# A hybrid decoder block on one core: recurrence gates as 64-row products, pooling by a scan, the mixer's scale on ScalarE

## The chip, the core and the metric

The kernel runs on one NeuronCore of a Trainium2 chip. A core has a matmul engine (TensorE, PE in the profile, with PEld for its weight loads), VectorE (DVE), ScalarE (ACT), GpSimd (POOL) and SyncE (SP), which here issues DMAs. Matmuls write to PSUM, from which VectorE and ScalarE read; everything else lies in SBUF, 128 partitions wide. The metric is the time of one launch in microseconds (us) on the device.

## The reference

One layer on x of 1024 tokens by 1024 channels, in float32. The projection `proj` (1536 columns) is cut into a pooling part (512), a recurrent part (512) and a gate branch (512):

```python
z = rms_norm(h, norm_mix_g[l]); proj = z @ w_in[l]
# pooling: four groups of 128 channels, trailing means over w = 2, 4, 8, 16 tokens
outs.append((c - c_lag) / count[None, :, None] - ug[:, :, g])      # c: running sum, c_lag: the same w tokens ago
y = jnp.einsum('bsgc,gcd->bsgd', d, pool_w) + pool_b
return y.reshape(B, S, D_POOL) * pool_scale
# recurrence: 8 heads of 64 channels, after a causal convolution of 4 taps
r = sigmoid(einsum('bshi,hij->bshj', uh, gate_a_w) + gate_a_b)
i = sigmoid(einsum('bshi,hij->bshj', uh, gate_x_w) + gate_x_b)
a = exp(LRU_C * r * log_sigmoid(lru_L)); b = sqrt(1 - a*a) * (i * u)   # h[t] = a[t] h[t-1] + b[t]
```

Then come `w_out` on both parts, an MLP of 4096 with squared ReLU, a gated embedding (`w_ple_gate`, `w_ple_proj`) and a final norm.

## The kernel before, in words

Channels lie on partitions and tokens along the free axis, so a tile is 128 channels by 1024 tokens. Every product is made of three matmuls per 128x128 block and 512 tokens: each operand is split into a high and a low part (`split`: ScalarE writes the high part, VectorE the low one), and `mm` runs high x high, high x low, low x high.

The stages in order of time: the norm and the first three projections (`ps_l`), nine more projections of eight blocks each (`ps_i`, by `project`, 48 matmuls each), with the gates (`ps_g`, `lru_gates`) and the mixer (`ps_p`, `pool_mix`) between them, the output projection (`ps_o`), the MLP (`ps_P`, by a Strassen-like scheme), and the gated embedding (`ps_e`, `ps_j`).

The recurrence works on four tiles `o` of 128 channels, two heads each, in two pairs. `conv` makes the tile `H[o]` and its split `B[4 + o]`. `lru_gates(pair)` multiplies it by the gate weights, which lie block-diagonally in 128x128 blocks (the two heads' 64x64 blocks, zeros elsewhere), once for gate a and once for gate x, and ScalarE takes the sigmoid of each from PSUM. `lru_scan` makes a and b of them (Exp, Tanh, Square, Sqrt on ScalarE) and runs the recurrence as one scan on VectorE. `pool_windows(g)` adds a tile to itself shifted by 1, 2, 4, 8 until the window is full.

PSUM has eight banks of 512 columns. `psum()` hands them out in turn: odd calls take a tile of 1024 columns from a pool of two (`pp`), even calls two banks of a pool of four (`pd`). A tile is reused once all of its readers are done, so a product waits for the readers of the one two of its kind before. The order on each engine is that of a scheduler which places the instructions of the program text; each engine then runs its own list strictly in order, held by semaphores. `LSETS` are the scratch tiles for the gates: first a's place (`ct`, gate x before that), then r (`rt`, gate a).

Weights come by DMA into `raw` tiles and are split ahead of use (`weights`, one block ahead); the small gate and mixer weights go through the two tiles `hl`.

Of the kernel before, what the change touches and what calls it, by code (L numbers as in the profile page):

```python
# [7 lines left out]
F32 = mybir.dt.float32  # L8
F32R = mybir.dt.float32r
AF = mybir.ActivationFunctionType  # L10
ALU = mybir.AluOpType

P = 128
S = 1024
D = 1024
DFF = 4096
HALF = 512
# [11 lines left out]
NLRU = 4  # L29
NPOOL = 4  # L30
# [7 lines left out]
COLS = {}  # L38
# [11 lines left out]
def block_kernel(  # L50
# [16 lines left out]
    nc = tc.nc  # L67
    pool = ctx.enter_context(tc.tile_pool(name="pool", bufs=1))
# [10 lines left out]
    T = [t_all[:, i] for i in range(6)]  # L79
# [10 lines left out]
    def space(name, n, dt, side="left"):  # L90

        spaces[name] = ExitStack()
        sb = spaces[name].enter_context(tc.tile_pool(name=name, bufs=1, side=side))
        return [sb.tile([P, S], dt, name=f"{name}{i}") for i in range(n)]
# [4 lines left out]
    def pairs(tiles):  # L99
        return list(zip(tiles[::2], tiles[1::2]))  # L100
# [13 lines left out]
    B = pairs(space("y", 12, F32R)) + pairs(space("y2", 4, F32R, "right"))  # L114

    def bank(name):
        return pd.tile([P, HALF], F32, tag="pd", name=name)

    def banks(name):
        return pp.tile([P, S], F32, tag="pp", name=name)  # L120
# [4 lines left out]
    def hl(i):  # L125
        return small[i // 2][:, HALVES[i % 2]]
# [3 lines left out]
    def psum(name, one=False):  # L130

        turn.append(name)
        if one or len(turn) % 2 == 1:
            return [(slice(0, S), banks(name))]
        return [(hs, bank(f"{name}_{hs.start}")) for hs in HALVES]

    def f32(ap):
        return ap.bitcast(F32)

    def col(name, i):  # L140
        c = COLS[name] + i
        return vecs[:, c : c + 1]
# [6 lines left out]
    def split(src, hi, lo, g=None, eng=None):  # L149

        if g is None:
            pin(nc.scalar.activation(hi, src, AF.Copy))  # L152
            pin((eng or nc.vector).tensor_tensor(lo, src, f32(hi), ALU.subtract))  # L153
        else:
            pin(nc.scalar.activation(hi, src, AF.Identity, scale=g))
            pin(nc.vector.scalar_tensor_tensor(lo, src, g, f32(hi), ALU.mult, ALU.subtract))  # L156
# [148 lines left out]
    def small_weights(name, raw):  # L305
        hi, lo = hl(2), hl(3)
        split(raw, hi, lo)
        return hi, lo

    def mm(parts, whi, wlo, zhi, zlo, first, last, only=None, more=False, held=False):  # L310
        outs = [
            (slice(hs.start + n, hs.start + min(n + HALF, w)), ps[:, n : min(n + HALF, w)])
            for hs, ps in parts
            for w in (hs.stop - hs.start,)
            for n in range(0, w, HALF)
            if only is None or hs.start + n == only.start
        ]
        for w, z in ((whi, zhi), (whi, zlo), (wlo, zhi)):
            for hs, ps in outs:
                ins = nc.tensor.matmul(  # L320
                    ps, w, z[:, hs],
                    start=first and z is zhi and w is whi,
                    stop=last and w is wlo,
                    skip_group_check=more,
                )
                if held:
                    tc.keep_in_program_order(ins)
                    held = False

    def kblk(t, k):  # L330
        return t[:, k * P : (k + 1) * P]


    vecs = pool.tile([P, NVEC], F32, name="vecs")
# [4 lines left out]
    ones_f = f32(ones)  # L339
# [3 lines left out]
    class Norm:  # L343
# [53 lines left out]
        def rstd(self, out, parts=None):  # L397


            for hs, o in parts or self.sums():  # L400
# [6 lines left out]
                nc.vector.reciprocal(few, few)  # L407
                nc.vector.transpose(r, few.unsqueeze(2).broadcast_to([P, n, 32]))

    def tables():  # L410

        one = ones_f[:, :16]
        tc.keep_in_program_order(
            nc.vector.tensor_tensor_scan(recip_t, one, one, 0.0, ALU.mult, ALU.add)
        )
        nc.vector.reciprocal(recip_t, recip_t)


        tc.keep_in_program_order(nc.vector.memset(T[5], 0.0))
        rv = T[5].rearrange("p (n a t c) -> p n a t c", n=2, a=2, t=2)  # L420
        for pair in range(2):
            for a in range(2):
                for par in range(2):
                    r = slice(64 * par, 64 * par + 64)
                    nc.sync.dma_start(rv[r, pair, a, :, r], gates[pair, a, par])


    norm = Norm("n0", T[0], T[1:3])
# [50 lines left out]
    def project(i):  # L479

        whi, wlo = weights()
        ps = psum(f"ps_i{i}")
        for k in range(NT):
            mm(ps, kblk(whi, k), kblk(wlo, k), *A[k], k == 0, k == NT - 1)
        return ps

    def normed(dst, parts):
        for hs, ps in parts:
            nc.vector.tensor_tensor(dst[:, hs], ps, R[:, hs], ALU.mult)

    def conv(o, ps):
        u, xb = (H[6], T[4])[o % 2], H[o]
        normed(u, ps)
        nc.scalar.activation(
            xb, u, AF.Identity, bias=col("conv_b", o), scale=col("conv_w", 4 * o + TAPS - 1)
        )
        for j in range(1, TAPS):
            nc.vector.scalar_tensor_tensor(
                xb[:, j:], u[:, : S - j], col("conv_w", 4 * o + TAPS - 1 - j), xb[:, j:],
                ALU.mult, ALU.add,  # L500
            )
        split(xb, *B[4 + o])

    LSETS = ((H[4], H[5], H[6]), (H[7], T[3], T[4]))

    gate_w, mix_w = {}, {}

    def ask_gates(pair):
        gate_w[pair] = small_weights(f"gw{pair}", T[5][:, pair * HALF : (pair + 1) * HALF])

    def ask_mix():
        raw = wp.tile([P, S], F32, tag="raw", name="pw_raw")[:, :HALF]
# [2 lines left out]

    def lru_gates(pair):

        hi, lo = gate_w[pair]
        for t in range(2):
            o = 2 * pair + t  # L520
            ct, rt, _ = LSETS[t]
            for a, (dst, b) in enumerate(((rt, "ga_b"), (ct, "gx_b"))):
                ps = psum(f"ps_g{a}{o}")
                mm(ps, kblk(hi, 2 * a + t), kblk(lo, 2 * a + t), *B[4 + o], True, True)
                for hs, part in ps:
                    nc.scalar.activation(dst[:, hs], part, AF.Sigmoid, bias=col(b, o))
            nc.vector.tensor_tensor(H[o], H[o], ct, ALU.mult)

    def lru_scan(pair):
# [23 lines left out]
    def pool_windows(g, ps):  # L553
        w = WINDOWS[g]
        u, *st = T[:3]
        if ps:
            normed(u, ps)
        cur, step, n = u, 1, 0
        while step < w:
            nxt = st[n % 2]  # L560
            nc.vector.tensor_tensor(nxt[:, step:], cur[:, step:], cur[:, : S - step], ALU.add)
            nc.vector.tensor_copy(nxt[:, :step], cur[:, :step])
            cur, step, n = nxt, 2 * step, n + 1
        nc.vector.tensor_tensor(cur[:, : w - 1], cur[:, : w - 1], recip_t[:, : w - 1], ALU.mult)
        nc.vector.tensor_tensor(cur[:, : w - 1], cur[:, : w - 1], u[:, : w - 1], ALU.subtract)
        nc.vector.scalar_tensor_tensor(
            cur[:, w - 1 :], cur[:, w - 1 :], 1.0 / w, u[:, w - 1 :], ALU.mult, ALU.subtract
        )
        split(cur, *B[g])

    def pool_mix(pair):
        whi, wlo = mix_w[0]
        for t in range(2):
            g = 2 * pair + t
            ps = psum(f"ps_p{g}")
            mm(ps, kblk(whi, g), kblk(wlo, g), *B[g], True, True)
            for hs, part in ps:
                nc.vector.tensor_scalar(
                    T[5][:, hs], part, col("pool_b", g), col("pool_s", g), ALU.add, ALU.mult
                )  # L580
            split(T[5], *B[g])

    conv(0, ps_l[0])
    conv(1, ps_l[1])
    ask_gates(0)
    conv(2, ps_l[2])
    conv(3, project(0))
    pool_windows(0, project(1))
    lru_gates(0)
    ask_gates(1)  # L590
    pool_windows(1, project(2))
    ps = project(3)
    normed(T[0], ps)
    lru_scan(0)
    lru_gates(1)
    ask_mix()
    pool_windows(2, None)
    ps = project(4)
    pool_mix(0)
    pool_windows(3, ps)  # L600
    gate_out(0, project(5))
    lru_scan(1)
    gate_out(1, project(6))
    pool_mix(1)
    gate_out(2, project(7))
    gate_out(3, project(8))
# [3 lines left out]
    for o in range(NT):  # L610
        whi, wlo = weights()
        nc.sync.dma_start(H[o], xT[o * P : (o + 1) * P, :])
        ps = psum(f"ps_o{o}")
        for k in range(NT):
            mm(ps, kblk(whi, k), kblk(wlo, k), *B[k], k == 0, k == NT - 1)
        z = T[o % 2]
# [79 lines left out]
    for o in range(0, NT, 2):  # L696
        t = o // 2
        for i in range(2):
            split(H[o + i][:, FIRST], *half(B[t], i), col("g_mlp", o + i))
    for o in range(1, NT, 2):  # L700
        t = o // 2
# [412 lines left out]
```

## Time and profile before

| what | value |
|---|---|
| time, median of 3 runs | 976.52 us (976.5 to 977.01) |
| profiled execution, its own time | 977.54 us |
| its span, first to last instruction | 975.5 us |
| TensorE busy | 964.8 us (99%), 4472 matmuls |
| VectorE busy | 757.0 us (78%), 885 instructions |
| ScalarE busy | 442.7 us (45%), 528 instructions |
| GpSimd busy | 99.1 us (10%) |
| mean granted TensorE clock | 0.998 |

A row of the timeline gives the start in us from the span's start, the duration, the engine, the line of the kernel, the operation, output and input tiles, shape, and how many instructions were merged; in brackets stands the idle time before it and what ended that. A row of the chain gives start, duration, engine, tile and line. A row of the windows gives from:to, length, and for PE, PEld, DVE, ACT and POOL busy time and count, then granted clock, DMA share and GB/s.

### The profile page before, as it was taken

How to read it: one execution, taken by the hardware profiler on the slowest of the kernel's cores; microseconds unless marked ns; L12 is line 12 of the kernel's file. 1: busy time of each engine (PE TensorE's matmuls, PEld its weight loads, DVE VectorE, ACT ScalarE, POOL GpSimd, SP SyncE). 2: the span in 40 equal slices, each digit the busy share in tenths (PEclk: the TensorE clock that was granted, in tenths of full speed). 3: DMA queues.
4: the chain of work that ended last, by engine and by line, in shares of the span. 5: the costliest groups of instructions: out<-in, count | busy, mean ns of one | idle time of the engine just before them, and what ended most of it. 6: DMA issues, size and time to landing. Idle time of an engine off the chain costs nothing.

```text
span 975.5 us, 11507 instructions
## 1 busy us (share of the span) xinstructions
PE 964.8 (99%) x4472; PEld 805.2 (83%) x4472; DVE 757.0 (78%) x885; ACT 442.7 (45%) x528; POOL 99.1 (10%) x72
## 2 busy tenths in 40 slices
PE   9999999999999999999999999999999999999996
PEld 7888888888788888888888888888888888888996
DVE  7999995449887777677777899879775669784976
ACT  7377643336543343334333544444343337552534
POOL 0000000002523322332331000000000000000210
PEclk9999999999999999999999999999999999999999
DMA  6301243110245345434533897356532341031122
GB/s 231 105 23 33 87 151 107 45 43 30 82 152 201 119 140 177 159 119 160 196 119 137 307 368 254 110 194 202 174 118 90 108 151 44 3 127 44 44 87 87
DMA packets 46198, 125.04 MB, mean 128 GB/s; under 512 B 5312, under 2 KB 7360, under 8 KB 46144
## 3 DMA queue, kind: packets, MB, share of 16 engines
q1 hardware_dynamic: 46000, 124.27, 36.9%
q8 instruction: 35, 0.57, 0.2%
q14 instruction: 19, 0.16, 0.1%
q10 hardware_dynamic: 144, 0.04, 0.0%
HBM read 90.74 MB, written 33.55 MB: 127 GB/s over the span
## 4 chain that ended last, share of the span: by engine, by line
PE 95%; DVE 3%; ACT 1%; DMA 1%; issue 0%; SPq 0%; DVEq 0%
PE ps_P_u L320 31%; PE ps_P_d L320 31%; PE ps_i L320 10%; PE ps_o L320 9%; PE ps_e L320 8%; PE ps_l L320 3%; PE ps_g L320 1%; PE ps_j L320 1%; PE ps_p L320 1%; DVE h L968 1%; DMA h<-in_xT 1%; DVE a L153 1%; DVE a L156 0%; DVE t L984 0%; DVE wu_lo L153 0%
## 5 line engine op out<-in xcount | busy, mean ns | idle before, releaser
L320 PE MATMUL ps_P_d<-a,wd_P_hi 128*128 128x512 f32 x880 | 271.1, 389 | 0.0
L320 PEld LDWEIGHTS ps_P_d<-a,wd_P_hi 128*128 128x128 f32 x880 | 165.2, 188 | 34.4
L320 PE MATMUL ps_P_d<-a,wd_P_lo 128*128 128x512 f32 x440 | 171.3, 389 | 0.0
L320 PE MATMUL ps_P_u<-a,wu_hi 128*128 128x512 f32 x512 | 157.7, 389 | 0.0
L320 PE MATMUL ps_P_u<-y,wu_hi 128*128 128x512 f32 x384 | 118.1, 389 | 0.0
L320 PEld LDWEIGHTS ps_P_u<-a,wu_hi 128*128 128x128 f32 x512 | 96.1, 188 | 19.9
L659 DVE TENSOR_TENSOR t<-t,ps_P_u 128x512 f32<-128x512 f32 (+1 forms) x80 | 62.6, 784 | 47.9 <-PE ps_P_u L320 47.7
L320 PE MATMUL ps_P_u<-a,wu_lo 128*128 128x512 f32 x256 | 99.6, 389 | 0.0
L320 PEld LDWEIGHTS ps_P_d<-a,wd_P_lo 128*128 128x128 f32 x440 | 82.6, 188 | 17.4 <-DVE wd_P_lo L153 0.3
L320 PEld LDWEIGHTS ps_P_u<-y,wu_hi 128*128 128x128 f32 x384 | 72.1, 188 | 14.9
L320 PE MATMUL ps_i<-a,wi_hi 128*128 128x512 f32 x288 | 77.1, 389 | 0.0
L320 PE MATMUL ps_P_u<-y,wu_lo 128*128 128x512 f32 x192 | 74.8, 390 | 0.4 <-DVE wu_lo L153 0.4
L153 DVE TENSOR_TENSOR a<-wd,a 128x1024 fp32r<-128x1024 f32 x56 | 67.1, 1219 | 5.2 <-ACT a L152 4.1
L152 ACT ACTIVATE a<-wd 128x1024 fp32r<-128x1024 f32 x56 | 58.8, 1057 | 21.2 <-PE ps_P_d L320 10.2
L320 PE MATMUL ps_o<-y,wo_hi 128*128 128x512 f32 x256 | 68.4, 389 | 0.0
L320 PEld LDWEIGHTS ps_i<-a,wi_hi 128*128 128x128 f32 x288 | 54.1, 188 | 11.2
L152 ACT ACTIVATE wu_hi<-wu 128x1024 fp32r<-128x1024 f32 x24 | 25.5, 1062 | 78.3 <-PE ps_P_u L320 43.9
L152 ACT ACTIVATE wu_hi<-wu_raw 128x1024 fp32r<-128x1024 f32 (+1 forms) x25 | 25.3, 1011 | 78.2 <-PE ps_P_u L320 44.8
L320 PEld LDWEIGHTS ps_P_u<-a,wu_lo 128*128 128x128 f32 x256 | 48.0, 188 | 10.0
L320 PEld LDWEIGHTS ps_o<-y,wo_hi 128*128 128x128 f32 x256 | 48.0, 188 | 10.0
L152 ACT ACTIVATE wd_P_hi<-wd 128x1024 fp32r<-128x1024 f32 x24 | 25.4, 1060 | 58.2 <-PE ps_P_d L320 58.0
L153 POOL TENSOR_TENSOR wg_lo<-wg_raw,wg_hi 128x1024 fp32r<-128x1024 f32 x4 | 9.9, 2478 | 408.7 <-DVE h L953 382.1
(224 smaller groups left out, 1634.2 us busy)
## 6 DMA issues: line engine op xcount, KB each, us to landing
wd<-act SPq DMA_DIRECT2D x56, 512.0 KB, 5.6
act<-t SPq DMA_DIRECT2D x32, 512.0 KB, 4.3
wu_raw<-in_w_up SPq DMA_DIRECT2D x16, 512.0 KB, 3.7
wu<-in_w_up SPq DMA_DIRECT2D x16, 512.0 KB, 4.6
act<-wu SPq DMA_DIRECT2D x16, 512.0 KB, 4.5
wd<-in_w_down SPq DMA_DIRECT2D x16, 512.0 KB, 6.2
h<-in_xT SPq DMA_DIRECT2D x15, 512.0 KB, 4.3
wg_raw<-in_w_gate SPq DMA_DIRECT2D x12, 512.0 KB, 3.3
```

The lines of the kernel that those rows point to most:

```text
L152: pin(nc.scalar.activation(hi, src, AF.Copy))
L153: pin((eng or nc.vector).tensor_tensor(lo, src, f32(hi), ALU.subtract))
L320: ins = nc.tensor.matmul(ps, w, z[:, hs], start=first and z is zhi and w is whi, stop=last and w is wlo, skip_group_check=more,)
L659: (eng or nc.vector).tensor_tensor(to, to if y is None else y, x, ALU.add)
L968: nc.vector.scalar_tensor_tensor(hv, hv, col("g_fin", o), rfin[:, hs], ALU.mult, ALU.mult)
```

## The change

Three things. The gate weights are packed so that one 64-row product per head gives both gates: weights `[64 rows, 128 columns]` with gate a in one half of the columns and gate x in the other (swapped for the second head), so that the two heads of a tile use rows 0-63 and 64-127 of the array and write to two PSUM tiles. Each PSUM tile then holds gate a in 64 of its partitions and gate x in the others, so the sigmoids go by halves of 64 partitions. The weights need half the columns (512 for all eight heads), one DMA, no zeroing and one split. Pooling over 4, 8 and 16 tokens becomes a running sum by a scan: state + u[t] - u[t - w], after a short scan for the first w tokens. The mixer's `(x + b) * s` becomes `x * s + b * s` in one ScalarE instruction, with `b * s` made once.

```diff
+    pool_bs = pool.tile([P, NPOOL], F32, name="pool_bs")
...
-        tc.keep_in_program_order(nc.vector.memset(T[5], 0.0))
-        rv = T[5].rearrange("p (n a t c) -> p n a t c", n=2, a=2, t=2)
...
-                    nc.sync.dma_start(rv[r, pair, a, :, r], gates[pair, a, par])
+        nc.sync.dma_start(T[5][:, FIRST], gates)
+        nc.vector.tensor_tensor(pool_bs, vecs[:, c_b : c_b + NPOOL], vecs[:, c_s : c_s + NPOOL], ALU.mult)
...
+    HEADS = slice(0, 64), slice(64, P)
-    def ask_gates(pair):
-        gate_w[pair] = small_weights(f"gw{pair}", T[5][:, pair * HALF : (pair + 1) * HALF])
+    def ask_gates():
+        gate_w[0] = small_weights("gw", T[5][:, FIRST])
...
     def lru_gates(pair):
-        hi, lo = gate_w[pair]
+        hi, lo = gate_w[0]
         for t in range(2):
             o = 2 * pair + t
             ct, rt, _ = LSETS[t]
-            for a, (dst, b) in enumerate(((rt, "ga_b"), (ct, "gx_b"))):
-                ps = psum(f"ps_g{a}{o}")
-                mm(ps, kblk(hi, 2 * a + t), kblk(lo, 2 * a + t), *B[4 + o], True, True)
-                for hs, part in ps:
-                    nc.scalar.activation(dst[:, hs], part, AF.Sigmoid, bias=col(b, o))
+            zhi, zlo = B[4 + o]
+            ps = [psum(f"ps_g{h}{o}") for h in range(2)]
+            halves = [
+                [(hs.start + n, x[:, n : n + HALF]) for hs, x in parts for n in range(0, hs.stop - hs.start, HALF)]
+                for parts in ps
+            ]
+            for n, (w, z) in enumerate(((hi, zhi), (hi, zlo), (lo, zhi))):
+                for (at, x0), (_, x1) in zip(*halves):
+                    for r, x in zip(HEADS, (x0, x1)):
+                        nc.tensor.matmul(
+                            x, w[r, o * P : (o + 1) * P], z[r, at : at + HALF], start=n == 0, stop=n == 2
+                        )
+            for dst, b, rows in ((rt, "ga_b", HEADS), (ct, "gx_b", HEADS[::-1])):
+                for h, r in enumerate(rows):
+                    for hs, part in ps[h]:
+                        nc.scalar.activation(
+                            dst[HEADS[h], hs], part[r], AF.Sigmoid, bias=col(b, o)[r]
+                        )
...
-        cur, step, n = u, 1, 0
-        while step < w:
-            nxt = st[n % 2]
-            nc.vector.tensor_tensor(nxt[:, step:], cur[:, step:], cur[:, : S - step], ALU.add)
-            nc.vector.tensor_copy(nxt[:, :step], cur[:, :step])
-            cur, step, n = nxt, 2 * step, n + 1
+        cur = st[g % 2]
+        if w == 2:
...
+        else:
+            nc.vector.tensor_tensor_scan(cur[:, :w], ones_f[:, :w], u[:, :w], 0.0, ALU.mult, ALU.add)
+            nc.vector.tensor_tensor_scan(
+                cur[:, w:], u[:, w:], u[:, : S - w], cur[:, w - 1 : w], ALU.add, ALU.subtract
+            )
...
-                nc.vector.tensor_scalar(
-                    T[5][:, hs], part, col("pool_b", g), col("pool_s", g), ALU.add, ALU.mult
-                )
+                nc.scalar.activation(
+                    T[5][:, hs], part, AF.Identity, bias=pool_bs[:, g : g + 1], scale=col("pool_s", g)
+                )
...
     conv(1, ps_l[1])
-    ask_gates(0)
+    ask_gates()
...
     lru_gates(0)
-    ask_gates(1)
     pool_windows(1, project(2))
```

How instructions move, at the two places of the first gate pair. The first is ScalarE's list from the sigmoids of the first gate tile on. `ps_g_0`, `ps_g_512` are the two banks of a `pd` product, `ps_g` without such a number is a 1024-column product, `y_130` is the high part of the fourth convolved tile. Before:

```order
L526 ACTIVATE h<-ps_g_0_609,vecs 128x512 [waits PE_49]
L526 ACTIVATE h<-ps_g_512_610,vecs 128x512 [waits PE_49]
L526 ACTIVATE h<-ps_g_619,vecs 128x1024 [waits PE_49]
L526 ACTIVATE t<-ps_g_0_628,vecs 128x512 [waits PE_49]
L526 ACTIVATE t<-ps_g_512_629,vecs 128x512 [waits PE_49]
L152 ACTIVATE y_130<-h 128x1024 [waits DVE_49,Activation_49]
L526 ACTIVATE h<-ps_g_638,vecs 128x1024 [waits PE_49]
```

and in the changed kernel, the same place:

```order
L539 ACTIVATE h<-ps_g_0_603,vecs 64x512 [waits PE_49]
L539 ACTIVATE h<-ps_g_512_604,vecs 64x512 [waits PE_49]
L539 ACTIVATE h<-ps_g_605,vecs 64x1024 [waits PE_49]
L152 ACTIVATE y_130<-h 128x1024 [waits DVE_49,Activation_49]
L539 ACTIVATE h<-ps_g_0_603,vecs 64x512
L539 ACTIVATE h<-ps_g_512_604,vecs 64x512
L539 ACTIVATE h<-ps_g_605,vecs 64x1024
```

Each gate product is now read twice, and the second reading of the first one (`ps_g_0_603`, `ps_g_512_604`) stands behind the split into `y_130`. The second place is TensorE's list for the second gate tile of the pair and the start of the next projection. Before:

```order
L320 MATMUL ps_g_0_628<-y_123,hl_136 128x512
L320 MATMUL ps_g_512_629<-y_123,hl_136 128x512
L320 MATMUL ps_i_0_655<-a,wi_hi 128x512 [waits Activation_49]
L320 MATMUL ps_g_638<-y_123,hl_136 128x512 [waits DVE_49]
L320 MATMUL ps_g_638<-y_123,hl_136 128x512
L320 MATMUL ps_g_638<-y_124,hl_136 128x512 x2
L320 MATMUL ps_g_638<-y_123,hl_136 128x512 x2
L320 MATMUL ps_i_512_656<-a,wi_hi 128x512 [waits Activation_49]
```

and in the changed kernel:

```order
L533 MATMUL ps_g_0_625<-y_123,hl_136 128x512
L533 MATMUL ps_g_512_626<-y_123,hl_136 128x512
L533 MATMUL ps_g_627<-y_123,hl_136 128x512 [waits DVE_49]
L533 MATMUL ps_g_627<-y_123,hl_136 128x512
L533 MATMUL ps_g_627<-y_124,hl_136 128x512 x2
L533 MATMUL ps_g_627<-y_123,hl_136 128x512 x2
L320 MATMUL ps_i_0_653<-a,wi_hi 128x512 [waits PE_49,Activation_49]
```

In this tile the six matmuls of rows 0-63 (`ps_g_0_625`, `ps_g_512_626`) stand ahead of the six of rows 64-127 (`ps_g_627`); in the other three tiles the two halves alternate. The projection's first matmul no longer stands inside the gates.

More of the change, by code (lines that the diff above doesn't have):

```diff
@@ L408, in rstd @@
                 nc.vector.transpose(r, few.unsqueeze(2).broadcast_to([P, n, 32]))
+    pool_bs = pool.tile([P, NPOOL], F32, name="pool_bs")
+    c_b, c_s = COLS["pool_b"], COLS["pool_s"]
     def tables():
@@ L416, in tables @@
         nc.vector.reciprocal(recip_t, recip_t)
-        tc.keep_in_program_order(nc.vector.memset(T[5], 0.0))
-        rv = T[5].rearrange("p (n a t c) -> p n a t c", n=2, a=2, t=2)
[L421 to L424, printed above, removed]
-                    nc.sync.dma_start(rv[r, pair, a, :, r], gates[pair, a, par])
+        nc.sync.dma_start(T[5][:, FIRST], gates)
+        nc.vector.tensor_tensor(pool_bs, vecs[:, c_b : c_b + NPOOL], vecs[:, c_s : c_s + NPOOL], ALU.mult)
     norm = Norm("n0", T[0], T[1:3])
@@ L557, in pool_windows @@
             normed(u, ps)
-        cur, step, n = u, 1, 0
-        while step < w:
-            nxt = st[n % 2]
-            nc.vector.tensor_tensor(nxt[:, step:], cur[:, step:], cur[:, : S - step], ALU.add)
-            nc.vector.tensor_copy(nxt[:, :step], cur[:, :step])
-            cur, step, n = nxt, 2 * step, n + 1
+        cur = st[g % 2]
+        if w == 2:
+            nc.vector.tensor_tensor(cur[:, 1:], u[:, 1:], u[:, : S - 1], ALU.add)
+            nc.vector.tensor_copy(cur[:, :1], u[:, :1])
+        else:
[3 more added lines that the diff above has]
+            )
         nc.vector.tensor_tensor(cur[:, : w - 1], cur[:, : w - 1], recip_t[:, : w - 1], ALU.mult)
@@ L1071 @@
     conv = np.asarray(conv_w)[0].reshape(TAPS, NLRU, P).transpose(2, 1, 0).reshape(P, NLRU * TAPS)
+    gx_b = np.roll(cols(gate_x_b), 64, axis=0)
     vec = np.concatenate(
@@ L1074 @@
             cols(norm_mix_g), cols(norm_mlp_g), cols(norm_ple_g), cols(norm_final_g), cols(pool_b),
-            cols(pool_scale), conv, cols(conv_b), cols(gate_a_b), cols(gate_x_b), cols(lru_L),
+            cols(pool_scale), conv, cols(conv_b), cols(gate_a_b), gx_b, cols(lru_L),
             cols(b_ple_gate),
@@ L1079 @@
     )
-    gates = np.stack([np.asarray(g)[0].reshape(2, 2, 2, 64, 64) for g in (gate_a_w, gate_x_w)])
-    gates = gates.transpose(1, 0, 3, 4, 2, 5)
+    ga, gx = (np.asarray(g)[0].reshape(NLRU, 2, 64, 64) for g in (gate_a_w, gate_x_w))
+    gates = np.stack([np.stack([ga[:, 0], gx[:, 0]], 2), np.stack([gx[:, 1], ga[:, 1]], 2)])
+    gates = gates.transpose(0, 2, 1, 3, 4)
     wu = np.asarray(w_up)[0].reshape(NT // 2, 2, P, NPAIR, 2, P).transpose(3, 2, 4, 1, 0, 5)
@@ L1093 @@
         "pool_w": c(np.asarray(pool_w)[0].transpose(1, 0, 2)).reshape(P, NPOOL * P),
-        "gates": c(gates),
+        "gates": c(gates).reshape(P, NLRU * P),
         "w_out": tiles(np.asarray(w_out)[0]),
```

## Prediction

> **What bounds the kernel now.** I read the page first, then the waits of TensorE alone up to 250 us, then the chain that ended last, and last the timeline of the two places where the recurrence's gates are computed.
>
> ```profile
> PE 964.8 (99%) x4472; PEld 805.2 (83%) x4472; DVE 757.0 (78%) x885; ACT 442.7 (45%) x528; POOL 99.1 (10%) x72
> PE ps_l L320 <- DVE a L156: 0.3, 1, 0.3
> 62.53 4.08 PE ps_g L320 x18
> 66.83 1.36 PE ps_g L320 x6
> 68.19 21.53 PE ps_i L320 x95
> 89.73 5.44 PE ps_g L320 x24
> 95.17 10.88 PE ps_i L320 x48
> ```
>
> TensorE works 99% of the span, and up to 250 us its matmuls wait once for input data, 0.3 us at the start. The chain shows what it does in the region of the change: 24 gate matmuls for heads' pair 0 (62.5 to 68.2), two projections, 24 gate matmuls for pair 1, the next projection, with nothing between them. One 128x512 matmul takes 5.44/24 = 0.2267 us. So a microsecond less of TensorE there is worth one at the end, but only if TensorE doesn't begin to wait; and a wait that appears there is lost in full, since nothing later in the chain makes it up. The other engines in that stretch:
>
> ```profile
> 50.00:75.00 25.00, 25.00 (x112) 20.71 (x111) 25.00 (x27) 19.24 (x21) 0.00 (x0) 1.00 0.06 22
> 75.00:100.00 25.00, 25.00 (x112) 20.67 (x112) 23.81 (x28) 19.32 (x20) 0.00 (x0) 1.00 0.16 53
> ```
>
> VectorE (fourth column: 25.00, then 23.81 of 25 us) and ScalarE (19.2 of 25) are nearly full too. They run just ahead of TensorE, so the reader should expect that a faster gate product runs into one of them.
>
> **What leaves VectorE, and why it is worth nothing.**
>
> ```profile
> 112.00 1.22 DVE L561 TENSOR_TENSOR t<-t 128x1023 f32<-128x1023 f32 x1
> 113.14 1.22 DVE L153 TENSOR_TENSOR y<-t,y 128x1024 fp32r<-128x1024 f32 x1
> 87.04 2.29 DVE L544 TENSOR_TENSOR_SCAN h<-h 128x1024 f32<-128x1024 f32 x1
> 115.41 1.52 DVE L578 TENSOR_SCALAR t<-ps_p,vecs 128x512 f32<-128x512 f32 x2
> ```
>
> An add of 1023 columns occupies VectorE 1.14 us (112.00 to 113.14), a scan of 1024 2.29 us. Windows 4, 8 and 16 had 2, 3 and 4 adds (2.3, 3.4, 4.6 us, plus small copies) and now have one scan each, about 2.4 us with its short head: 0, 1.0 and 2.2 us less. The mixer's shift and scale, four tiles of about 1.4 us, go to ScalarE. That is some 9 us off VectorE, nearly all behind 96 us where TensorE waited for nothing: worth 0. So is the zeroing of the gate weights' tile and the eight small DMAs. The one gates DMA now stands on SP's queue ahead of the fourth x tile, but the wait it could cause has cover:
>
> ```profile
> 22.49 1.15 ACT L155 ACTIVATE a<-h,vecs 128x1024 fp32r<-128x1024 f32 x1 [1.21 <-DMA h<-in_xT]
> 31.44 1.28 DVE L383 TENSOR_TENSOR hl<-t,hl 128x512 fp32r<-128x512 f32 x2
> 35.56 0.40 PE L384 MATMUL n_ps<-hl,ones 128*128 128x512 f32 x1
> ```
>
> The last x tile lands at 22.5, its sums are split by 32.7 and TensorE takes them up at 35.6: 2.8 us of slack. I take 0, with 0.3 either way.
>
> **The gate products.** There are still 48 matmuls of 512 columns (12 for each of four tiles o), now with 64 rows each. Where they alternate between rows 0-63 and 64-127, two can run at once: 6 x 0.2267 = 1.36 us for a tile instead of 2.72. By the order of the built program this holds for three of the four: for the second tile of pair 0 all six of one half come first, then the six of the other. TensorE's own gain would be 3 x 1.36 = 4.1 us. The trace of before has no 64-row matmul. Its bounds are 0.2267 us for two (both run together) and 0.4534 (one after the other). Weight loads don't stand against the lower one:
>
> ```profile
> 916.83 2.90 PE L320 MATMUL ps_e<-a 128*128 128x256 f32 x24
> 919.57 0.39 PE L384 MATMUL n_ps<-ple,ones 128*128 128x512 f32 x1
> ```
>
> 24 matmuls of 256 columns, each with its own load, take 2.74 us, 0.114 each, so two loads fit in one 0.2267. I take the lower bound.
>
> **What gives it back.** A gate tile's bank is now read twice, because each bank holds 64 rows of both gates: eight 1024-column tiles become sixteen of 64 rows (24 ScalarE instructions for 12), and rows don't shorten an instruction that goes by columns. The projection that follows pair 0 (ps_i in two banks) takes over the first gate tile's banks. Before, their two readers were the first two of the sigmoids; now the last readers stand behind the split of y_130. ScalarE and VectorE there:
>
> ```profile
> 63.19 1.28 ACT L526 ACT_TABLE_LOAD   x1
> 64.49 2.27 ACT L526 ACTIVATE h<-ps_g,vecs 128x512 f32<-128x512 f32 x3
> 65.17 1.22 DVE L489 TENSOR_TENSOR t<-ps_i,rstd 128x1024 f32<-128x1024 f32 x1
> 66.31 1.27 DVE L498 SCALAR_TENSOR_TENSOR h<-t,vecs,h 128x1021 f32<-128x1021 f32 x1
> 66.64 1.27 ACT L526 ACTIVATE t<-ps_g,vecs 128x512 f32<-128x512 f32 x2
> 67.78 1.08 ACT L152 ACTIVATE y<-h 128x1024 fp32r<-128x1024 f32 x1
> 68.73 1.14 ACT L526 ACTIVATE h<-ps_g,vecs 128x1024 f32<-128x1024 f32 x1
> 254.28 0.50 PE L320 MATMUL ps_P_u<-y,wu_lo 128*128 128x512 f32 x1 [0.45 <-DVE wu_lo L153]
> 254.62 0.63 PE L320 MATMUL ps_P_u<-y,wu_hi 128*128 128x512 f32 x2
> ```
>
> Pair 0, step by step. The split of y_130 needs the last tap of the convolution, which VectorE ends at 66.31 + 1.27 = 67.58 in both kernels (its order up to there is the same). So the split starts at 67.60, the next sigmoid 0.95 later (67.78 to 68.73) at 68.55. A 512-column sigmoid lasts 0.70 (two starts 0.57 apart end after 1.27), so the first bank is free at 69.25. A matmul released by a wait starts 0.04 later and loses 0.11 (254.28 to 254.62 is 0.34 for one of 0.2267): as if it had started at 69.40. Before, the 96 matmuls up to 89.73 began in effect at 89.73 - 96 x 0.2267 = 67.97. **+1.43 us**, and not a function of how fast the gates are: done by 67.8 (the second half waits for a bank until VectorE has read ps_i at 66.39, then six matmuls), they wait 1.5 us.
>
> Pair 1 starts at T = 91.2. ScalarE before:
>
> ```profile
> 89.31 1.06 ACT L152 ACTIVATE wi_hi<-wi_raw 128x1024 fp32r<-128x1024 f32 x1 [1.14 <-PE ps_i L320]
> 90.39 1.28 ACT L526 ACT_TABLE_LOAD   x1
> 91.69 2.27 ACT L526 ACTIVATE h<-ps_g,vecs 128x512 f32<-128x512 f32 x3
> 93.84 1.28 ACT L526 ACTIVATE t<-ps_g,vecs 128x512 f32<-128x512 f32 x2
> 89.56 5.60 PE L320 MATMUL ps_g<-y,hl 128*128 128x512 f32 x24
> 91.50 1.22 DVE L489 TENSOR_TENSOR t<-ps_i,rstd 128x1024 f32<-128x1024 f32 x1
> ```
>
> The next projection again takes the first gate tile's banks, read first and fourth among the sigmoids. In the built program the table load itself now waits for the first bank's ninth matmul, which starts 4 x 0.2267 after T and ends 0.39 later: T + 1.30. Then 0.04, the load 1.28, three sigmoids 2.15 (91.69 to 93.84), the fourth 0.70, 0.04 and 0.11: T + 5.62, against 5.44 before. **+0.18 us.** The second tile needs another bank, which VectorE's read of the last projection (ps_i) frees: 91.50 + 1.22 = 92.7 before. It stands behind the scan that ScalarE feeds, and ScalarE now has 4.3 us of sigmoids more in pair 0, of which its gaps (it was 77% busy there) hide most; I expect it 1 to 2 us later. It takes over only from T + 4.2 = 95.4 on (six more matmul pairs of 1.36 us end at T + 5.6), and then a us costs a us.
>
> Changing between full and half height may add a gap in which the array runs empty. The nearest row is the tail of one matmul, 0.39 - 0.23 = 0.16 us; it counts only on entering pair 1 (elsewhere TensorE waits anyway). Bounds 0 and 0.16, I take 0.1. The Trainium skill, TensorEngine Tiling (Array Packing), section Tiling Modes, says that changing the mode drains TensorE; no row of before shows it, and it gives no figure.
>
> Sum: 1.43 + 0.18 + 0.1 = +1.7 us. Behind 95 us I find no new wait: VectorE has less to do, and ScalarE's four new readers free banks that TensorE wants ten microseconds later. The profiled execution took 977.54 (span 975.5), 1.0 over the median of the runs shown; a difference carries over: 976.52 + 1.7 = 978.2.
>
> **The rivals.** About 0.2%, 1.95 us, is what a measurement of this kernel can tell from no change.
>
> Slower: the halves don't overlap (the change doesn't do what it says). Pair 0 still ends by ScalarE (its 24 matmuls in series end at 67.97), +1.43; in pair 1 the ninth matmul starts at 8 x 0.2267, 0.91 later, and everything behind it: 1.43 + 0.18 + 0.91 = +2.5, 979.0. If also a half's next load can't hide behind its own matmul, a step costs
>
> ```profile
> 36.03 0.19 PEld L385 LDWEIGHTS n_ps<-hl,ones 128*128 128x128 f32 x1
> ```
>
> 0.19 more, 0.42: the unpaired tile then ends at 62.53 + 18 x 0.42 = 70.1, 0.7 past 69.4, the ninth matmul of pair 1 starts 4 x 0.19 = 0.8 later, and the sum is 1.7 + 0.7 + 0.8 = +3.2, 979.7. For it: nothing here shows such loads; against: full-height loads hide. It decides from a pair time of about 0.29 us on (1.95 - 1.7 = 0.25, over four pairs). The skill's TensorE: Matmul & The Clock Gate, Part 3, lets a load pass a running matmul only where the row groups differ, which would speak for 979.7, and measures row tiles as concurrent, which speaks against 979.0. Chance 0.23.
>
> Slower: the gaps cool TensorE's clock.
>
> ```profile
> 1.31 4.64 PE L432 MATMUL ps_l<-ones 128*128 128x512 f32 x10 [1.31 <-DVE ones L338]
> ```
>
> The first ten matmuls, after an idle start, took 0.46 each, 2.4 us more than warm ones. The gaps here are 1.2 and 1.5 us, then about 2; each such relapse costs about 2.4: 980.6. Against: after the waits of 0.3 to 0.5 us in this trace rows go on at full rate, but it has none of 1.5. Chance 0.07.
>
> Faster: the gates' time is really saved. 4.1 us less, 972.4, if no bank is waited for. The Trainium skill, TensorEngine Tiling (Array Packing), Theoretical Speedup, gives up to 2x for a contraction of 64 or less, which would be 5.4 us of 10.88, 971.1; the same page under PSUM Bottleneck says that tiling doesn't speed up the evacuation. The rows speak for the second. Chance 0.07.
>
> **How the numbers follow.** The forecast has 0.63: about 978.2, its own range 977.3 to 978.9 (0.3 for the start, 0.1 for the drain, and VectorE or ScalarE late by a few tenths). Some 0.45 of chance lies within 1.95 us and 0.18 above. Slower: 0.18 + 0.23 + 0.07 = 0.48; same 0.45; faster 0.07. The range 977.0 to 979.9 leaves out the faster case, the cold clock and the edges.
>
> **What would show it.** Right: in the profile after, TensorE waits for ScalarE before the first ps_i matmul behind each pair, about 1.5 us in pair 0; ps_g matmuls of two halves start together; the last ps_g of pair 0 is done before 68; ps_o starts at about 156.7 instead of 155.0, and all behind it keeps that distance. Wrong: a first ps_i matmul before 68.5 (banks free earlier), ps_g taking 5 us of TensorE again (no overlap), 0.46 us matmuls behind a gap, or a new wait of TensorE behind 96 us.

## The result, and the profile after

The changed kernel takes 999.75 us (median of 4, 999.49 to 1000.97) against 976.51 (976.49 to 977.01) for the kernel before on the same chip: ratio 1.0239, 95% interval 1.0221 to 1.0257. It is slower by 23.2 us where +1.7 was forecast, and 999.75 is far outside the range. The profiled run took 999.52 us, its span is 997.7.

First TensorE's busy time on the page, then its two new waits, and the timeline of the gates of pair 0:

```profile
PE 983.7 (99%) x4472; PEld 804.3 (81%) x4472; DVE 745.2 (75%) x866; ACT 457.3 (46%) x545; POOL 99.2 (10%) x72
```

```profile
PE ps_i L320 <- ACT h L539: 2.5, 2, 1.4
PE ps_g L533 <- DVE t L489: 1.8, 2, 1.3
```

```profile
63.27 3.00 PE L533 MATMUL ps_g<-y,hl 64*128 64x512 f32 x18
66.78 1.65 PE L533 MATMUL ps_g<-y,hl 64*128 64x512 f32 x6 [0.52 <-DVE t L489]
69.83 0.74 PE L320 MATMUL ps_i<-a,wi_hi 128*128 128x512 f32 x2 [1.40 <-ACT h L539]
```

The forecast wait is there (1.40 us before the first `ps_i` behind pair 0), and so is the overlap of the halves. But TensorE is busy 18.9 us longer (983.7 against 964.8) with the same 4472 matmuls, though 48 of them now run in pairs. Some rows of the chain of the kernel before, at the borders of the stages:

```profile
133.25 21.76 PE ps_i L320 x96
155.01 87.04 PE ps_o L320 x384
262.76 285.70 PE ps_P_u L320 x1259
854.01 5.44 PE ps_e L320 x24
```

and of the changed kernel:

```profile
139.27 22.40 PE ps_i L320 x96
161.67 87.89 PE ps_o L320 x384
270.28 290.78 PE ps_P_u L320 x1260
561.06 313.60 PE ps_P_d L320 x1344
874.66 5.45 PE ps_e L320 x24
```

The distance grows from border to border: 6.66 us at the start of `ps_o`, 7.52 at the long row of `ps_P_u`, 12.60 at its end (561.06 against 262.76 + 285.70 = 548.46), where `ps_P_d` begins, and 20.65 at `ps_e`. Stages that the change doesn't touch lose the most, and no wait stands there. The groups of instructions show how: line, engine, tiles, shape and count, then busy us, mean ns of one, idle us before. Before:

```profile
L320 PE MATMUL ps_P_d<-a,wd_P_hi 128*128 128x512 f32 x880 | 271.1, 389 | 0.0
L320 PE MATMUL ps_P_u<-a,wu_hi 128*128 128x512 f32 x512 | 157.7, 389 | 0.0
L320 PE MATMUL ps_P_u<-y,wu_hi 128*128 128x512 f32 x384 | 118.1, 389 | 0.0
```

After:

```profile
L320 PE MATMUL ps_P_d<-a,wd_P_hi 128*128 128x512 f32 x880 | 276.6, 396 | 0.0
L320 PE MATMUL ps_P_u<-a,wu_hi 128*128 128x512 f32 x512 | 161.0, 396 | 0.0
L320 PE MATMUL ps_P_u<-y,wu_hi 128*128 128x512 f32 x384 | 118.4, 390 | 0.0
```

In these rows every matmul that moves `a` through the array takes 7 ns more; those that move `y` hardly change (389 to 390). The mean of one includes the overlap with the next; the pace itself is read from the chain, where 96 matmuls of a projection took 21.76 us before (0.2267 each) and take 22.40 now (0.2333). There are 2688 matmuls of 512 columns with moving `a`, and 96 of `ps_e` that take their weights from `a` (389 ns before, 395 after): 2784 x 0.0067 = 18.6 us. It begins with the first projections (six matmuls in 1.40 us instead of 1.36 from 12 us on), long before the first gate.

What changed for them is where their weights lie. `pool_bs`, 16 bytes a partition, padded to 32, was allocated ahead of the weight tiles: these, `y` and `hl` moved up by 32 bytes, `a` did not. In the kernel before, `a`, the weight tiles and `y` lie a multiple of 256 bytes apart (by the sizes in the program, the tiles from the start of `a` to the weights fill 70912 bytes, 277 x 256). My theory was therefore: a matmul is slower when its weights and its moving tile lie at another distance. The rival: half-array matmuls, or the changed program as a whole, slow TensorE everywhere.

### The profile page after: what moved, and what is told of

Read it like the earlier page. It is cut to its first block, busy times and chain, and to the rows that moved or that the text cites. A ratio compares the mean times of both kernels' runs of the same rounds, so it can differ in the third digit from the quotient of the medians.

```text
span 997.7 us, 11510 instructions
## 1 busy us (share of the span) xinstructions
PE 983.7 (99%) x4472; PEld 804.3 (81%) x4472; DVE 745.2 (75%) x866; ACT 457.3 (46%) x545; POOL 99.2 (10%) x72
## 4 chain that ended last, share of the span: by engine, by line
PE 92%; DVE 5%; ACT 2%; DMA 0%; issue 0%; SPq 0%; DVEq 0%; ACTq 0%
PE ps_P_d L320 31%; PE ps_P_u L320 31%; PE ps_o L320 9%; PE ps_e L320 8%; PE ps_i L320 8%; PE ps_l L320 3%; DVE h L498 1%; PE ps_j L320 1%; PE ps_p L320 1%; DVE h L986 1%; DMA h<-in_xT 0%; ACT h L539 0%; DVE y L153 0%; DVE t L489 0%; DVE a L153 0%
## 5 line engine op out<-in xcount | busy, mean ns | idle before, releaser
L320 PE MATMUL ps_P_d<-a,wd_P_hi 128*128 128x512 f32 x880 | 276.6, 396 | 0.0
L320 PE MATMUL ps_P_d<-a,wd_P_lo 128*128 128x512 f32 x440 | 174.0, 396 | 0.0
L320 PE MATMUL ps_P_u<-a,wu_hi 128*128 128x512 f32 x512 | 161.0, 396 | 0.0
L320 PEld LDWEIGHTS ps_P_u<-y,wu_hi 128*128 128x128 f32 x384 | 72.1, 188 | 15.4
L320 PE MATMUL ps_i<-a,wi_hi 128*128 128x512 f32 x288 | 80.5, 401 | 2.5 <-ACT h L539 2.5
```

The costliest lines, as they stand in the source:

```text
L320: ins = nc.tensor.matmul(ps, w, z[:, hs], start=first and z is zhi and w is whi, stop=last and w is wlo, skip_group_check=more,)
```

## The experiments

**Kernel after, 64 bytes instead of 32.**

```diff
-    pool_bs = pool.tile([P, NPOOL], F32, name="pool_bs")
+    pool_bs = pool.tile([P, 16], F32, name="pool_bs")[:, :NPOOL]
```

> Kernel after, with pool_bs made 64 bytes wide instead of 16 (padded to 32), so that the weight tiles lie a whole 64 bytes further than in the kernel before instead of 32. Placement theory (a matmul whose weights lie 32 bytes off its moving tile, modulo 64, takes 0.2333 us instead of 0.2267): with moving a the mean of a 128x512 matmul is back at 389 ns, ps_o starts about 158 to 159 instead of 161.7, and the time is 978 to 981 us (976.5 + 1.7 for the waits behind the gates + up to 1.7 for the clock's fall behind the first of them). Rival (half-array matmuls, or the larger program, slow TensorE everywhere): 396 ns with moving a, 998 to 1001 us.

Measured: 999.05 us (998.73 to 1001.78). The theory as I had put it, modulo 64, failed (96 matmuls of a projection still take 22.40 us); the rival stood.

**Kernel before with the 32 bytes alone.**

```diff
+    gap = pool.tile([P, 4], F32, name="gap")
+    nc.gpsimd.memset(gap, 0.0)
     def tables():
```

> Kernel before, with nothing but a 16-byte tile more (zeroed once by GpSimd) where the change puts pool_bs; all that is allocated behind it, the weight tiles and y, moves by 32 bytes, a stays. Placement theory: 128x512 matmuls with moving a take 396 ns instead of 389, those with moving y stay at 389; 994 to 998 us without any of the change's own work. Rival (the gates' half-array matmuls or the program slow TensorE): 976 to 977.5 us.

Measured: 997.02 us (996.61 to 997.29), ratio 1.0208 (1.0193 to 1.0223). The groups of this kernel:

```profile
L320 PE MATMUL ps_P_d<-a,wd_P_hi 128*128 128x512 f32 x880 | 276.6, 396 | 0.0
L320 PE MATMUL ps_P_u<-a,wu_hi 128*128 128x512 f32 x512 | 161.0, 396 | 0.0
L320 PE MATMUL ps_P_u<-y,wu_hi 128*128 128x512 f32 x384 | 118.4, 390 | 0.0
```

They are the rows of the changed kernel to the digit. An unused tile does this, without any of the change's own work: the rival falls.

**Kernel before, `a` and the weights both moved by 32 bytes** (the same tile, allocated just ahead of `a`).

> Kernel before, with the same 16-byte tile ahead of a: a, the weight tiles and y all move by 32 bytes, and stand to one another as in the kernel before. If what counts is where the weights lie relative to the moving tile: 976 to 977.5 us, 389 ns with moving a. If what counts is that one of them starts on 64 bytes by itself: 994 us or more, with a, y or both at 396 ns.

Measured: 978.76 us (977.68 to 980.26), ratio 1.0022 (1.0012 to 1.0031). A projection's 96 matmuls take 21.76 us, as before: the distance counts, not where `a` lies by itself. The chain shows where a small rest is:

```profile
132.90 21.76 PE ps_i L322 x96
154.66 87.87 PE ps_o L322 x384
```

`ps_o` takes 87.87 us instead of 87.04. Of the eight pairs of tiles that it moves, the last two (`y2` in the kernel) are allocated from the other end of the memory: this edit moves the weights by 32 bytes and leaves these tiles where they are. The timeline inside `ps_o` shows it. Each of these rows begins a block of six matmuls: the sixth, seventh and eighth block of one product, then the first of the next (the rows of the low weights between them are left out, and the second block of the next product begins at 177.83):

```profile
172.28 1.07 PE L322 MATMUL ps_o<-y,wo_hi 128*128 128x512 f32 x4
173.64 1.10 PE L322 MATMUL ps_o<-y,wo_hi 128*128 128x512 f32 x4
175.04 1.09 PE L322 MATMUL ps_o<-y,wo_hi 128*128 128x512 f32 x4
176.44 1.09 PE L322 MATMUL ps_o<-y,wo_hi 128*128 128x512 f32 x4
```

The sixth block takes 1.36 us, as in the kernel before; the seventh and eighth, which move `y2`, take 1.40, six times 0.2333; the one right behind them still takes 1.39, those from 177.83 on 1.36 again. That is about 0.1 us a product, and `ps_o` has eight: the 0.83 us are the same effect, on the tiles that did not move along. The changed kernel has it too (87.89). The rest of the 2 us stays open.

**Kernel before, weights and `y` moved by 128 bytes.** (A tile of 32 words at the same place.)

> Kernel before with a tile of 128 bytes ahead of the weight tiles and y, a in its place. 32 bytes (994.7 us of span) and 64 bytes (the kernel after with the 64-byte tile) both slow the matmuls with moving a; both moved by 32 bytes do not. If the distance of weights from moving tile counts modulo 128 bytes, 389 ns and 976 to 978 us; if modulo 256 or more, 394 to 396 ns with moving a and 993 to 998 us.

Measured: 995.59 us (995.54 to 996.12), ratio 1.0191 (1.0177 to 1.0205), 395 ns with moving `a`.

**The same by 256 bytes.**

> As the run before this one with 256 bytes. If the distance counts modulo 256 or less: 389 ns with moving a, ps_o at 87.0 us as in the kernel before, 976 to 977.5 us. If only the very distance of the kernel before is fast (or the modulus is 512 or more): 993 to 998 us.

Measured: 976.74 us (976.19 to 977.64), ratio 0.9998 (0.9989 to 1.0007), and in the chain:

```profile
132.84 21.76 PE ps_i L320 x96
154.59 87.04 PE ps_o L320 x384
```

**Kernel before, `a` alone moved by 16 bytes** (views of `a` from its fifth column on, 256 bytes added to the tile).

> Kernel before with all of a's views 16 bytes further and the weight tiles and y 256 bytes further, so that a alone leaves the common multiple of 256. If any distance other than a multiple of 256 bytes slows a matmul: 394 to 396 ns with moving a, 993 to 998 us, y at 389. If only distances of 32 bytes or more do: 389 ns and 976 to 977.5 us.

Measured: 991.12 us (991.09 to 991.27), ratio 1.0142 (1.0129 to 1.0155). 96 matmuls take 22.24 us, 0.2317 each: 5.0 ns more, three quarters of what 32 bytes cost. This was between my two cases.

**Kernel before, `y` alone moved by 32 bytes.**

```diff
         sb = spaces[name].enter_context(tc.tile_pool(name=name, bufs=1, side=side))
+        if name == "y":
+            gap = sb.tile([P, 8], F32, name="gap")
```

> Kernel before with 32 bytes ahead of y alone: y (and hl behind it) moves against the weight tiles, while a and the weight tiles stay where they are. If the distance of moving tile to weights is what counts, the slow matmuls change sides: 128x512 matmuls of ps_o and ps_P_u with moving y go from 389 to 394 to 396 ns, those with moving a stay at 389; 384 of ps_o and 576 of ps_P_u at 6.7 ns each give 6.4 us, 982 to 984 us. If a is special (its own address, or its size): y stays at 389 to 391 ns and the time at 976 to 978.5 us.

Measured: 983.16 us (982.91 to 983.36), ratio 1.0061 (1.0048 to 1.0074). The slow matmuls changed sides:

```profile
L323 PE MATMUL ps_P_d<-a,wd_P_hi 128*128 128x512 f32 x880 | 270.9, 389 | 0.0
L323 PE MATMUL ps_P_u<-y,wu_hi 128*128 128x512 f32 x384 | 120.5, 395 | 0.0
L323 PE MATMUL ps_o<-y,wo_hi 128*128 128x512 f32 x256 | 69.9, 395 | 0.0
```

So it is a matter of the two tiles of one matmul. The distances tried, modulo 256 bytes: 0 gives 0.2267 us; `a` 16 bytes on gives 0.2317; weights 32, 64 and 128 bytes on all give 0.2333.

**Kernel after, every tile at its address of the kernel before.**

```diff
-    pool_bs = pool.tile([P, NPOOL], F32, name="pool_bs")
+    sp = pool.tile([P, 8, NLRU], F32, name="sp")
+    pool_bs = sp[:, 7]
```

> Kernel after with pool_bs put into an unused part of the tile sp, so that every tile lies where it lay in the kernel before; all instructions stay. Placement theory: 389 ns with moving a, the waits behind the gates as in the kernel after (1.4 and about 1.2 us) and the clock at 0.5 for some 3 us behind pair 0: 978 to 981 us, with ps_o starting 2 to 4 us later than in the kernel before. Rival (the change slows TensorE by something else besides): over 985 us.

Measured: 982.06 us (981.26 to 982.4), ratio to before 1.0050 (1.0036 to 1.0064), a microsecond above the range expected and far below the rival's. The same instructions at other addresses: 17.7 us less than the changed kernel (18.3 when each is taken against the kernel before of its own chip). What is left is the change's own work, and its chain shows it:

```profile
69.53 23.53 PE ps_i L320 x96
93.06 1.37 PE ps_g L533 x9
98.94 11.17 PE ps_i L320 x48
159.07 87.04 PE ps_o L320 x384
```

`ps_o` starts 4.06 us later than before. 23.53 us for 96 matmuls is 1.77 over 21.76: the granted clock fell behind pair 0, and not behind pair 1. In the windows (granted clock is the third number from the right):

```profile
65.86:69.27 3.41, 1.65 (x6) 1.03 (x6) 3.41 (x5) 2.58 (x3) 0.00 (x0) 1.00 0.00 0
69.27:72.68 3.41, 3.15 (x7) 2.48 (x8) 3.41 (x6) 3.33 (x6) 0.00 (x0) 0.50 0.24 77
93.16:96.58 3.42, 1.82 (x15) 1.16 (x15) 3.42 (x3) 2.62 (x4) 0.00 (x0) 1.00 0.00 0
96.58:99.99 3.41, 2.60 (x16) 1.82 (x17) 3.41 (x4) 3.33 (x5) 0.00 (x0) 1.00 0.11 20
```

**The gates alone**, pooling and mixer as before, same addresses.

> Only the gates of the change (half-array products, their layout, ScalarE's reads), with the pooling and the mixer as before and every tile at its address of the kernel before. If the gates are all that is left of the loss at equal addresses: the time of the whole change at these addresses, 980.5 to 983 us, with ps_o 3 to 5 us later and one or two stretches at a granted clock of 0.5 around 68 to 104 us. If pooling and mixer hold part of it (the wait for VectorE's read of the fourth projection, which stands behind pooling work): 977 to 979.5 us.

Measured: 981.66 us (980.33 to 985.07), ratio 1.0048 (1.0036 to 1.0061). TensorE's waits:

```profile
PE ps_i L320 <- ACT h L536: 2.5, 2, 1.4
PE ps_g L530 <- DVE t L554: 1.3, 1, 1.3
```

The gates alone hold all that is left; here the clock stays at 0.5 from 68 to 75 us, and the 96 matmuls take 24.70 us.

**Pooling and mixer alone**, gates as before, same addresses.

> Only the pooling by scans and the mixer's shift and scale on ScalarE, with pool_bs in the unused part of sp, gates as before, every tile at its address of the kernel before. Costed at nothing: TensorE waits nowhere in the recurrence, ps_o starts at 154.5 to 155.3 us and the time is 976 to 977.5 us. If the scans hold TensorE (a bank read late behind a scan of 2.3 us): a wait of ps_g or ps_i of 0.5 us or more and 977.5 to 979 us.

Measured: 979.75 us (978.37 to 981.23), ratio 1.0029 (1.0020 to 1.0039), and the profiled run is the fastest of the ten. The median is above both ranges expected, the profiled run within the second. `ps_o` starts at 156.56 in it. VectorE's timeline, and the matmuls that wait for it:

```profile
88.14 2.29 DVE L548 TENSOR_TENSOR_SCAN h<-h 128x1024 f32<-128x1024 f32 x1
91.58 2.29 DVE L548 TENSOR_TENSOR_SCAN h<-h,t 128x1024 f32<-128x1024 f32 x1
93.78 1.20 DVE L493 TENSOR_TENSOR t<-ps_i,rstd 128x1024 f32<-128x1024 f32 x1
95.04 1.66 PE L320 MATMUL ps_g<-y,hl 128*128 128x512 f32 x6 [1.22 <-DVE t L493]
```

In the kernel before, VectorE read the fourth projection (L489) at 91.50, between the two recurrence scans of pair 0; here the scheduler has put it behind both, and the second gate tile of pair 1 waits 1.22 us for that bank. I had costed this edit at nothing. Alone it costs 1.5 us at `ps_o` and 2.7 in the medians (the difference stays open); with the new gates, which move VectorE's list again, nothing is added.

**Kernel after with 64 bytes, ScalarE's reads in order of banks.**

```diff
-            for dst, b, rows in ((rt, "ga_b", HEADS), (ct, "gx_b", HEADS[::-1])):
-                for h, r in enumerate(rows):
+            for h in range(2):
+                for dst, b, rows in ((rt, "ga_b", HEADS), (ct, "gx_b", HEADS[::-1])):
```

> As the kernel after with pool_bs of 64 bytes, and ScalarE's reads of a gate tile put in order of banks: both reads of the first half's banks come ahead of both reads of the second half's. Placement theory, with the wait behind the gates as predicted: the first ps_i behind each pair finds its banks free (the waits of 1.40 and 1.15 us are under 0.3 us), no stretch at a granted clock of 0.5 behind pair 0, and 975.5 to 977.5 us. Rival (the wait is not on these reads, but on VectorE or on ScalarE's whole queue): the gaps stay over 1 us and the time is that of the run with the 64-byte tile alone.

Measured: 996.43 us (995.45 to 998.09), against 999.05 for the kernel with 64 bytes alone; the time expected rested on the theory modulo 64 and was missed by 19 us. The wait and the fall of the clock behind pair 0 are gone (the first row: no idle time in brackets). They came back at pair 1:

```profile
68.47 1.20 PE L320 MATMUL ps_i<-a,wi_hi 128*128 128x512 f32 x4
95.22 2.92 PE L533 MATMUL ps_g<-y,hl 64*128 64x512 f32 x11 [2.27 <-DVE t L489]
```

```profile
94.00:96.00 2.00, 0.78 (x4) 0.69 (x6) 2.00 (x3) 1.98 (x4) 0.00 (x0) 0.81 0.00 0
96.00:98.00 2.00, 2.00 (x11) 1.14 (x7) 2.00 (x4) 1.96 (x3) 0.00 (x0) 0.50 0.00 0
```

**The same at the addresses of before, with VectorE's read of the fourth projection queued ahead of the scans.**

> As the run before this one, with two things more: ScalarE's reads of the gates in order of banks (which took the wait of 1.4 us behind pair 0 away, but let TensorE come 2.9 us earlier to pair 1, where it then waited 2.27 us for VectorE's read of the fourth projection behind two scans), and that read queued ahead of pair 0's scans. If those two queues are all that holds the gates: no wait over 0.6 us around the gates, no granted clock under 0.9 after 12 us, ps_o starts 1 to 3 us earlier than the kernel before, 973.5 to 976 us. If the scans' delay on VectorE comes back as a wait for y or for a bank later: 976 to 979 us.

Measured: 981.70 us (980.28 to 982.0), ratio 1.0045 (1.0032 to 1.0058), above both ranges expected. The wait of 2.27 us is gone and another took its place:

```profile
PE ps_i L320 <- ACT h L540: 3.7, 1, 3.7
PE ps_g L533 <- DVE t L489: 1.0, 1, 1.0
```

```profile
91.52 3.04 PE L533 MATMUL ps_g<-y,hl 64*128 64x512 f32 x24
98.30 0.73 PE L320 MATMUL ps_i<-a,wi_hi 128*128 128x512 f32 x2 [3.74 <-ACT h L540]
```

```profile
94.34 2.39 ACT L540 ACTIVATE h<-ps_g,vecs 64x512 f32<-64x512 f32 x3
97.56 2.40 ACT L540 ACTIVATE h<-ps_g,vecs 64x512 f32<-64x512 f32 x3 [0.83 <-DVE h L561]
```

The 24 gate matmuls of pair 1 now run through in 3.04 us, and the projection behind them waits 3.74 for ScalarE's sigmoids: 6.8 us from gate to projection, 5.4 before. The scheduler had not kept the order of banks there: the first three sigmoids take 2.39 us, more than three of 512 columns (0.7 at most for each), so one of 1024 columns is among them. And the fourth, at 97.56, had waited 0.83 us for VectorE's first scan, which now runs behind that read, from 95.24 on. The clock fell twice (68 to 72 and 99 to 103 us). No version here beats the kernel before.

## Why the prediction was wrong

**The duration of a matmul was carried over.** The step that failed is "One 128x512 matmul takes 5.44/24 = 0.2267 us": the sum used it for all of the changed kernel, and "all behind it keeps that distance" hung on it. The new tile of 16 bytes stands in the diff, and its place ahead of the weights in the program; there was no term for what it moves. Measured: 17.7 us of the 23.2 (changed kernel less the one at equal addresses), 20.3 when the 32 bytes are put into the kernel before. Shown by eight runs: the 32 bytes alone bring the loss, equal addresses take it away, 256 bytes bring none, and it follows the distance of weights to moving tile. Without it the time would still lie above the range, at 982.06, for the reasons that follow.

**The gates, pair 0.** Mechanism right, size near. By the starts in the timeline, from the first gate matmul of pair 0 to the first of pair 1, the kernel before took 62.37 to 89.56 = 27.19 us; the run at equal addresses 62.49 to 92.99 = 30.50. Of these 3.31 us more, 1.59 is the clock (the 96 matmuls from 69.53 on took 23.46, 1.70 over 21.76, less the 0.11 at a wait's end): +1.7 is left against +1.43 forecast.

**The gates, pair 1.** +0.18 forecast, +0.63 measured (92.99 to 109.95 against 89.56 to 105.89, where the mixer's matmuls start). ScalarE's four sigmoids were counted as 2.85 us; from 95.79 to the release at 98.9 they took 3.1, and the table load began 0.2 later than worked out. VectorE's read came late as feared: a wait of 1.60 us, mostly hidden behind ScalarE's.

**The cold clock** had a chance of 0.07, and it came true, once in the changed kernel: 12 matmuls behind pair 0 took 4.46 us instead of 2.80. The price was taken as 2.4 us from the start of the kernel; one fall cost about 1.6. At equal addresses it and the two terms make 1.6 + 1.7 + 0.6 = 3.9 us; the run was 0.1 late at the first gate matmul already (62.49 against 62.37), and together that is the 4.06 at `ps_o`. The drain of 0.1 can't be told apart in it. My ground against it, that rows go on at full rate behind waits of 0.3 to 0.5 us, said nothing on 1.4.

**The halves overlap.** Right: 24 matmuls of 64 rows in 3.04 us where nothing holds them (24 full ones in 5.60 in the same view before); the rival that they don't is out. That this saves nothing was right too: the old product's length covered what ScalarE and VectorE need, and each wait taken away (bank order, read order) came back as another one. The Trainium skill, TensorEngine Tiling (Array Packing), under PSUM Bottleneck, says that tiling doesn't make the evacuation faster; these rows agree, and here the evacuation even took more instructions (with the gates alone ScalarE is busy 452.3 us in 539 instructions, 442.7 in 528 before).

**Pooling and mixer at nothing.** Wrong by themselves (+2.7 us, of which 1.5 at `ps_o` by the order on VectorE), without effect beside the gates. That TensorE waits for nothing there was true of the kernel before; I had not followed which read falls behind which scan in the new order. Behind the waits of pair 1, the last of which ends at 99.94 in the changed kernel, there is no new wait, as forecast; the matmuls themselves were slower.

## What to carry to other kernels

Before forecasting, compare where the tiles lie as well as in which order instructions run: a small tile allocated ahead of matmul operands can shift weights against moving data and change the pace of every matmul that reads both. When unrelated stages slow down by a few per cent with no wait in sight, compare the mean of one instruction by its moving tile, and test with an unused tile of the same size. A product that hides the reading of its banks is not shortened for free: count the readers first, and whether the gap that opens lowers the clock.

## What the runs showed of the hardware

- A 128x512 matmul of this kernel's operands takes 0.2267 us when weights and moving tile start a multiple of 256 bytes apart, 0.2317 with the moving tile 16 bytes further, 0.2333 with the weights 32, 64 or 128 bytes further. Not tried: other distances, and other types. Moving both by 32 bytes leaves the matmuls on `a` as they were; the 0.83 us that `ps_o` then takes more lie on the tiles that did not move along. Why the distance matters no run shows.
- The granted clock falls to 0.5 for some 3.4 us (changed kernel, 70.7 to 74.1; last kernel above, 68.7 to 72.1), and once for twice that (gates alone). It fell behind a single wait of 0.96 us (last kernel, pair 0), of 2.27 (order of banks with 64 bytes, pair 1), of 3.74 (last kernel, pair 1), and of 0.52 and 1.40 together (changed kernel, pair 0), and did not behind 1.26 and 1.15 (changed kernel, pair 1) or 1.60 and 0.81 (equal addresses, pair 1). The length of a wait alone doesn't decide it.
- Two things hold for all seven falls in these traces ahead of the kernels' ends. Each begins 18, 19, 26 or 27 whole stretches of 3.413 us after the clock first rose to full. And in the stretch just before it TensorE did 20 to 38% of the work that fits into one, where a full matmul of 512 columns counts as 0.2267 us and one of 64 rows as half of that; in every other stretch at full clock between 8 and 900 us it did 40% or more. In the windows of the run at equal addresses, the six matmuls of 64 rows before 69.27 make 20%, and the clock fell; the stretch up to 96.58 has 41%, and it stayed. The one stretch at 0.5 with as little (gates alone, 33%) was followed by a second one at 0.5. This is read from the traces and fits all of them; no run was made to test it. The Trainium skill, TensorE: Matmul & The Clock Gate, Part 1, speaks of a window of about 3.4 us that runs by itself and of a fall after an idle one. The length and the fixed steps agree; here a stretch that was only partly idle was enough.
